# Two sets of transpose DMAs issued from GpSimd's queue, a double block with block sums at the end of branch 2, and a shorter last root

## The chip, the cores and the metric

One core of a Trainium2 chip runs the whole program. The times are device microseconds of that core from one launch. The kernel before has a median of 1646.37 us over three runs (1646.34 to 1649.3). The profile is of one further execution, which took 1648.74 us.

## The reference, cut to what matters

One layer of a hybrid block on x of 256 tokens by 2048 channels, all in float32.

```
h    = rmsnorm(x) ; proj = h @ w_in   -> q, k, v, u, z, xbc, dt, 3 gates (2048 x 13856)
att  = windowed attention(q, k, v)          # 256 x 1024
pool = multi-scale means of u, mixed        # 256 x 1024
y    = Mamba-2 scan(xbc, dt)                # 256 x 2048, four groups of 512 channels
ssm  = per-group rmsnorm(y * silu(z)) * ssm_norm_w
m    = s(g0)*(att @ w_attn_br) + s(g1)*(pool @ w_pool_br) + s(g2)*(ssm @ w_ssm_br)
x    = x + m @ w_out
x    = x + (silu(gu[:, :5632]) * gu[:, 5632:]) @ w_down     # gu = rmsnorm(x) @ w_gate_up
out  = rmsnorm(x) * final_w
```

## The kernel before, in words

Every matrix product is done as three TensorE products of rounded parts (L225 to L227, `three`): a float32 weight is cast to fp32r by ScalarE (`whi`, L142) and what the cast left over is computed by VectorE (`wlo`, L143). A **piece** is such a pair of tiles, 128 by 1024 numbers. It feeds twelve matmuls of 512 columns (two k rows, two token halves, three products). There are five buffers each for `whi` and `wlo`, so ScalarE and VectorE can run at most five pieces ahead of TensorE, and three buffers (`raw`) for the weights as they come from HBM, two pieces each. SP's queue issues the loads of `raw` (L153, L293), in program order, each as soon as a buffer is free.

A block of 512 output columns by all 256 tokens is made in one of two ways. `tokens_block` (L229 on) takes 8 pieces: 96 matmuls. `two_blocks` makes two such blocks at once. Of its eight pairs of k rows, two are done by block sums (Strassen's scheme with seven products: 21 matmuls instead of 24), the other six plainly. The block sums need more of VectorE: sums of weights (`vu`, `sraw`, L304 to L307) and of results (L361 to L364, and the adds after it).

A product's input must have its channels on the partitions, and what VectorE and ScalarE compute has its tokens there. `turn` (L487 to L516) changes that: 16 small DMAs (32 KB each, L497) carry a block into `mid`, two VectorE transposes of 32 by 32 squares follow (`tt`, L502), and then a split in rounded parts. Such a turn is made for the four groups of the state-space output (`y`, into `ssm`), for the four blocks of the merged branches (`m`, into `mp`), for the four residual blocks (`x`, into `x2p`) and for the feed-forward blocks. Before the change the 16 DMAs of `m` stand in GpSimd's queue and all others in SP's, among the weight loads.

The order on each engine comes from a scheduler that takes the program as written. Small jobs (`later`) wait in a list from which `side` takes one after each piece when enough time is held to be spare; `pause(5.0)` or `pause(12.0)` in that list keeps `turn`'s second half away from its first half. Each engine then runs its own instructions strictly in that order, so an instruction that waits holds up all behind it.

The stretch in question: branch 2's gates and products (`two_gates`, `gate`, `branch`), four z blocks (L1016 to L1033: `silu` of z, times `y`, sum of squares, root, scaling at L1027, then `turn`), branch 3's gates (`two_gates(2, 0)`, whose double block begins with a block-sum pair), and `two_branches`, which reads `ssm`. Later come w_out with `residual` (L1056) and the feed-forward part. The last lines (L1143 on) make the final root for each token half and store the output.

Of the kernel before, what the change touches and what calls it, by code (L numbers as in the profile page):

```python
# [10 lines left out]
F32 = mybir.dt.float32  # L11
# [6 lines left out]
D = 2048  # L18
# [53 lines left out]
def hybrid_block(ctx: ExitStack, tc: tile.TileContext, ins, out):  # L72
# [16 lines left out]
    def k4(shape, dt=F32, name="k4"):  # L89
        return work.tile([P, *shape], dt, tag="k4", name=name, bufs=22)  # L90
# [13 lines left out]
    def tr():  # L104
        return ps_tr.tile([P, NB], F32, tag="tr", name="tr")
# [17 lines left out]
    def pause(cost):  # L123
        tasks.append((lambda: None, cost))
# [124 lines left out]
    def plain_loads(w, k0, c0, cols):  # L249
        return lambda i, n: [(lambda r: r[:, :, :], rows(w, k0 + i, n, c0, cols))]  # L250
# [236 lines left out]
    def turn(block, k0, dst, scale=None, queue=sp):  # L487

        mid = k4([4, T, P], F32, "mid")
        dst.waiting.add(k0 // 4)

        def move():
            for i in range(4):
                for j in range(4):
                    queue.dma_start(mid[32 * j:32 * j + 32, i], block[32 * i:32 * i + 32, :, j * P:(j + 1) * P])  # L497

        def parts():
            tt = k4([4, SEQ], F32, "tt")  # L500
            for t in range(T):
                dve.transpose(  # L502
                    tt.rearrange("p k (t i s) -> p t i k s", t=T, i=4)[:, t],
                    mid[:, :, t].rearrange("p i (c k) -> p i k c", k=4),
                )
            if scale is None:
                hi, lo = dst.t[k0 // 4]
                split(tt, hi, lo)
            else:
# [409 lines left out]
    def two_gates(br, j):  # L919

        c0 = C_G + br * D + j * NB
        out = []
        for sums in two_blocks(h, h_forms, w_in, 0, (c0, c0 + NB), KD, False):
            sg = k4([T, NB], F32, "sg")
            for t, (q, more) in enumerate(sums):
                dve.tensor_tensor(more, q, more, ALU.add)
                act.activation(sg[:, t, :], more, AF.Sigmoid, scale=rstd1[:, t:t + 1])
            out.append(sg)
        return out
# [12 lines left out]
    def two_branches(j, sgs):

        for n, sums in enumerate(two_blocks(ssm, s_forms, ins["w_ssm_br"][0], 0, (j * NB, (j + 1) * NB), KD)):
            for t, (q, more) in enumerate(sums):
                dve.tensor_tensor(more, q, more, ALU.add)
                dve.tensor_tensor(more, more, sgs[n][:, t, :], ALU.mult)
                dve.tensor_tensor(m4[j + n][:, t, :], m4[j + n][:, t, :], more, ALU.add)
# [59 lines left out]
    sgs = two_gates(1, 1)  # L1008
    branch(1, 1, po, ins["w_pool_br"][0], sgs[0], [tr(), tr()])
    branch(1, 2, po, ins["w_pool_br"][0], sgs[1], [sm(), sm()])  # L1010
    branch(1, 3, po, ins["w_pool_br"][0], gate(1, 3))


    ssg = tiny([T, GROUPS], "ssg", 1)
    ssm = Parts(KD, "ssm")
    for g in range(GROUPS):  # L1016
        for t, a in enumerate(tokens_block(h, KD, plain_loads(w_in, 0, C_Z + g * NB, NB), NB)):
            sz = k2([NB], F32, "sz")
            act.activation(sz, a, AF.Silu, scale=rstd1[:, t:t + 1])
            dve.tensor_tensor(ys[g][:, t, :], ys[g][:, t, :], sz, ALU.mult)  # L1020
            junk = k2([NB], F32, "junk")
            act.activation(junk, ys[g][:, t, :], AF.Square, accum_out=ssg[:, t, g:g + 1])

        def finish(g=g):
            rstd = rsqrt(ssg[:, :, g], NB, [T], "rsg")
            for t in range(T):
                dve.tensor_scalar(ys[g][:, t, :], ys[g][:, t, :], rstd[:, t:t + 1], None, ALU.mult)  # L1027

        later(finish, 1.5)
        turn(ys[g], 4 * g, ssm, lambda k: norms[:, 0, k:k + 1])  # L1030

        if g == 0:
            s_forms = block_forms(ssm, (0, 1))  # L1033

    sgs = two_gates(2, 0)
    finish_tasks()
# [19 lines left out]
    def residual(j, accs):  # L1056
        for t, a in enumerate(accs):
            dve.tensor_tensor(x2[j][:, t, :], a, x2[j][:, t, :], ALU.add)
            junk = k2([NB], F32, "junk")
            act.activation(junk, x2[j][:, t, :], AF.Square, accum_out=ss2[:, t, j:j + 1])  # L1060
        turn(x2[j], 4 * j, x2p, lambda k: norms[:, 1, k:k + 1])
        if j == 0:
            forms.append(block_forms(x2p, (0, 1)))

# [78 lines left out]
    part = tiny([T], "part", 1)  # L1143
    dve.tensor_reduce(part, ss3, AX.X, ALU.add)
    dve.tensor_scalar(part, part, 1.0 / D, EPS, ALU.mult, ALU.add)
    out_v = out[0].rearrange("(t p) c -> p t c", p=P)
    for t in range(T):
        tok = slice(t * P, (t + 1) * P)
        o = acc()[:, :256]
        for k in range(nk):  # L1150
            hi, lo = wl[k // 4]
            three(o, f.hi(k)[:, tok], f.lo(k)[:, tok], hi[:, k % 4, :], lo[:, k % 4, :], k == 0, k == nk - 1)
        x_ = x2[3][:, t, 256:]
        dve.tensor_tensor(x_, o, x_, ALU.add)
        junk = k2([256], F32, "junk")
        ss = tiny([1], "ss_last")
        dve.scalar_tensor_tensor(junk, x_, 1.0, x_, ALU.mult, ALU.mult, accum_out=ss)
        rstd = rsqrt(ss, D, [1], "rs3", part[:, t:t + 1])
        dve.scalar_tensor_tensor(x_, x_, rstd, fw[7], ALU.mult, ALU.mult)
        sp.dma_start(out_v[:, t, 3 * NB + 256:], x_)  # L1160
        act.mul(x2[3][:, t, :256], x2[3][:, t, :256], rstd)
        act.dma_start(out_v[:, t, 3 * NB:3 * NB + 256], x2[3][:, t, :256])
        for j in range(3):
            if j == 1:
                act.mul(x2[j][:, t, :], x2[j][:, t, :], rstd)
                act.dma_start(out_v[:, t, j * NB:(j + 1) * NB], x2[j][:, t, :])
# [29 lines left out]
```

## Time and profile before

| what | value |
|---|---|
| median of three runs | 1646.37 us |
| the profiled execution | 1648.74 us |
| its span, first to last instruction | 1646.6 us |
| TensorE busy | 1626.4 us, 99% |
| VectorE busy | 1318.8 us, 80% |
| ScalarE busy | 898.2 us, 55% |
| GpSimd busy | 96.8 us, 6% |
| mean granted TensorE clock | 0.998 of 2.4 GHz |

TensorE's matmuls overlap, so its time is better counted in matmuls per stretch than in busy time. The counted stretches are in the rows below. Idle time stands in brackets behind an instruction, with what ended it.

### The profile page before, as it was taken

How to read it: one execution, taken by the hardware profiler on the slowest of the kernel's cores; microseconds unless marked ns; L12 is line 12 of the kernel's file. 1: busy time of each engine (PE TensorE's matmuls, PEld its weight loads, DVE VectorE, ACT ScalarE, POOL GpSimd, SP SyncE). 2: the span in 40 equal slices, each digit the busy share in tenths (PEclk: the TensorE clock that was granted, in tenths of full speed). 3: DMA queues.
4: the chain of work that ended last, by engine and by line, in shares of the span. 5: the costliest groups of instructions: out<-in, count | busy, mean ns of one | idle time of the engine just before them, and what ended most of it. 6: DMA issues, size and time to landing. Idle time of an engine off the chain costs nothing.

```text
span 1646.6 us, 20971 instructions
## 1 busy us (share of the span) xinstructions
PE 1626.4 (99%) x7689; PEld 1349.5 (82%) x7689; DVE 1318.8 (80%) x1738; ACT 898.2 (55%) x1190; POOL 96.8 (6%) x126
## 2 busy tenths in 40 slices
PE   8999999999999999999999999999999999999998
PEld 7888888888888888778888878888888888888887
DVE  5789898964786557688886799988879888888986
ACT  5467678644554457554545565554445555445553
POOL 1000001210220100002230000000000000000000
PEclk9999999999999999999999999999999999999999
DMA  8654566546566556566866666666666666666663
GB/s 250 204 159 146 166 196 205 179 158 200 161 224 212 197 185 212 155 233 203 265 221 191 202 211 226 206 215 215 204 205 193 219 214 217 205 203 199 216 212 103
DMA packets 214088, 328.83 MB, mean 200 GB/s; under 512 B 16253, under 2 KB 86145, under 8 KB 213985
## 3 DMA queue, kind: packets, MB, share of 16 engines
q1 hardware_dynamic: 209056, 317.77, 59.2%
q0 software_dynamic: 4176, 8.86, 1.9%
q8 instruction: 60, 0.98, 0.2%
q10 hardware_dynamic: 752, 0.86, 0.2%
q14 instruction: 44, 0.35, 0.1%
HBM read 313.25 MB, written 2.13 MB: 192 GB/s over the span
## 4 chain that ended last, share of the span: by engine, by line
PE 86%; SPq 4%; DMA 4%; DVE 3%; issue 1%; ACT 1%; DVEq 0%; ACTq 0%
PE acc L225 19%; PE acc L227 19%; PE acc L226 19%; PE acc L383 9%; PE acc L384 4%; SPq L497 4%; PE sm L226 2%; PE tr L227 2%; PE tr L226 2%; PE tr L225 2%; PE sm L225 2%; PE sm L227 2%; DVE wlo L143 1%; DMA raw<-in_w_gate_up_dram 1%; PE sm L868 1%
## 5 line engine op out<-in xcount | busy, mean ns | idle before, releaser
L143 DVE TENSOR_TENSOR wlo<-raw,whi 128x1024 fp32r<-128x1024 f32 (+2 forms) x500 | 600.2, 1215 | 155.8 <-ACT whi L142 154.7
L142 ACT CAST whi<-raw 128x1024 fp32r<-128x1024 f32 (+2 forms) x500 | 509.1, 1035 | 361.9 <-PE acc L227 244.3
L383 PE MATMUL acc<-h,whi 128*128 128x512 f32 x640 | 228.4, 400 | 0.0
L226 PE MATMUL acc<-wlo,x2p_hi 128*128 128x512 f32 x572 | 223.2, 390 | 1.2 <-DVE wlo L143 1.2
L225 PE MATMUL acc<-whi,x2p_hi 128*128 128x512 f32 x572 | 223.3, 390 | 0.0
L227 PE MATMUL acc<-whi,x2p_lo 128*128 128x512 f32 x572 | 223.0, 390 | 0.0
L226 PE MATMUL acc<-wlo,h 128*128 128x512 f32 (+1 forms) x508 | 195.5, 386 | 5.8 <-DVE wlo L143 5.7
L225 PE MATMUL acc<-whi,h 128*128 128x512 f32 (+1 forms) x508 | 196.9, 390 | 2.3 <-ACT whi L142 1.9
L227 PE MATMUL acc<-whi,h 128*128 128x512 f32 (+1 forms) x508 | 194.6, 386 | 0.0
L384 PE MATMUL acc<-h,wlo 128*128 128x256 f32 x640 | 180.3, 282 | 0.0
L142 ACT CAST whi<-sraw 128x1024 fp32r<-128x1024 f32 x84 | 88.1, 1049 | 121.8 <-PE acc L227 96.1
L383 PEld LDWEIGHTS acc<-h,whi 128*128 128x128 f32 x640 | 120.2, 188 | 30.1 <-issue 1.5
L143 DVE TENSOR_TENSOR wlo<-sraw,whi 128x1024 fp32r<-128x1024 f32 x84 | 102.6, 1221 | 45.4 <-ACT whi L142 45.2
L226 PEld LDWEIGHTS acc<-wlo,x2p_hi 128*128 128x128 f32 x572 | 107.4, 188 | 25.0 <-DVE wlo L143 2.3
L227 PEld LDWEIGHTS acc<-whi,x2p_lo 128*128 128x128 f32 x572 | 107.4, 188 | 23.0
L225 PEld LDWEIGHTS acc<-whi,x2p_hi 128*128 128x128 f32 x572 | 107.3, 188 | 23.0
L384 PEld LDWEIGHTS acc<-h,wlo 128*128 128x128 f32 x640 | 120.8, 189 | 1.8 <-issue 1.8
L226 PEld LDWEIGHTS acc<-wlo,h 128*128 128x128 f32 x508 | 95.8, 189 | 26.4 <-DVE wlo L143 7.2
L225 PEld LDWEIGHTS acc<-whi,h 128*128 128x128 f32 x508 | 95.6, 189 | 23.0 <-ACT whi L142 2.1
L227 PEld LDWEIGHTS acc<-whi,h 128*128 128x128 f32 x508 | 95.2, 188 | 19.4
L225 PE MATMUL acc<-whi,f_hi 128*128 128x512 f32 x244 | 95.3, 391 | 0.0
L227 PE MATMUL acc<-whi,f_lo 128*128 128x512 f32 x244 | 95.1, 390 | 0.0
(364 smaller groups left out, 2635.1 us busy)
## 6 DMA issues: line engine op xcount, KB each, us to landing
raw<-in_w_in_dram SPq DMA_DIRECT2D x80, 1024.0 KB, 5.3
raw<-in_w_gate_up_dram SPq DMA_DIRECT2D x132, 512.0 KB, 4.8
raw<-in_w_down_dram SPq DMA_DIRECT2D x62, 512.0 KB, 5.0
sraw<-in_w_gate_up_dram SPq DMA_DIRECT2D x44, 512.0 KB, 4.6
raw<-in_w_in_dram SPq DMA_DIRECT2D x43, 512.0 KB, 4.7
raw<-in_w_ssm_br_dram SPq DMA_DIRECT2D x24, 512.0 KB, 5.6
sraw<-in_w_down_dram SPq DMA_DIRECT2D x20, 512.0 KB, 5.0
raw<-in_w_attn_br_dram SPq DMA_DIRECT2D x8, 1024.0 KB, 5.1
```

What stands on the lines that cost most here:

```text
L142: a = act.copy(hi, src)
L143: b = dve.tensor_tensor(lo, src, hi.bitcast(F32), ALU.subtract)
L225: pe.matmul(o, lhsT=xh, rhs=yh, start=first, stop=False)
L226: pe.matmul(o, lhsT=xh, rhs=yl, start=False, stop=False)
L227: pe.matmul(o, lhsT=xl, rhs=yh, start=False, stop=last)
L383: pe.matmul(accs[c], lhsT=hi[:, j, cols], rhs=a.both(k), start=k == 0, stop=False)
L384: pe.matmul(accs[c][:, :SEQ], lhsT=lo[:, j, cols], rhs=a.hi(k), start=False, stop=k == KD - 1)
L497: queue.dma_start(mid[32 * j:32 * j + 32, i], block[32 * i:32 * i + 32, :, j * P:(j + 1) * P])
L868: pe.matmul(p[:, i * HD:(i + 1) * HD], lhsT=mt[:, i, :], rhs=xdt[:, i, :], start=True, stop=True)
```

## The change

Three edits. The turns of `y` and `x` issue their DMAs from GpSimd's queue, and the pause behind a GpSimd turn is 7.0 instead of 12.0. The last gate block of branch 2 and the first z block, two `tokens_block` products before, become one `two_blocks` product with block sums; the branch product that used that gate follows behind it and accumulates in other banks. For the last root ScalarE takes the sum of squares itself with scale and bias, and one VectorE step of the refinement is folded into a precomputed half.

```diff
@@ turn
         later(move)
-        pause(5.0 if queue is sp else 12.0)
+        pause(5.0 if queue is sp else 7.0)
         later(parts, 3.8)
...
+    def gate_of(sums):
+        sg = k4([T, NB], F32, "sg")
+        for t, (q, more) in enumerate(sums):
+            dve.tensor_tensor(more, q, more, ALU.add)
+            act.activation(sg[:, t, :], more, AF.Sigmoid, scale=rstd1[:, t:t + 1])
+        return sg
...
-    branch(1, 3, po, ins["w_pool_br"][0], gate(1, 3))
...
+    def gated(g, accs, in_place=False):
+        for t, a in enumerate(accs):
+            sz = a if in_place else k2([NB], F32, "sz")
             act.activation(sz, a, AF.Silu, scale=rstd1[:, t:t + 1])
             dve.tensor_tensor(ys[g][:, t, :], ys[g][:, t, :], sz, ALU.mult)
...
-        turn(ys[g], 4 * g, ssm, lambda k: norms[:, 0, k:k + 1])
+        turn(ys[g], 4 * g, ssm, lambda k: norms[:, 0, k:k + 1], pool)
...
+    both = two_blocks(h, h_forms, w_in, 0, (C_G + D + 3 * NB, C_Z), KD, False)
+    sg = gate_of(both[0])
+    for q, more in both[1]:
+        dve.tensor_tensor(more, q, more, ALU.add)
+    gated(0, [more for _, more in both[1]], True)
+    branch(1, 3, po, ins["w_pool_br"][0], sg, [tr(), tr()])
+    for g in range(1, GROUPS):
+        gated(g, tokens_block(h, KD, plain_loads(w_in, 0, C_Z + g * NB, NB), NB))
...
-        turn(x2[j], 4 * j, x2p, lambda k: norms[:, 1, k:k + 1])
+        turn(x2[j], 4 * j, x2p, lambda k: norms[:, 1, k:k + 1], pool)
...
+    halves = tiny([T], "halves", 1)
+    dve.tensor_scalar(halves, part, -0.5, None, ALU.mult)
...
-        rstd = rsqrt(ss, D, [1], "rs3", part[:, t:t + 1])
+        rstd, more = tiny([1], "rs3_r"), part[:, t:t + 1]
+        act.activation(rstd, ss, AF.Sqrt, scale=1.0 / D, bias=more)
+        half, q = tiny([1], "rs3_v"), tiny([1], "rs3_q")
+        dve.tensor_scalar(half, ss, -0.5 / D, halves[:, t:t + 1], ALU.mult, ALU.add)
+        dve.reciprocal(rstd, rstd)
+        dve.scalar_tensor_tensor(q, rstd, half, rstd, ALU.mult, ALU.mult)
+        dve.scalar_tensor_tensor(rstd, q, 1.5, rstd, ALU.add, ALU.mult)
```

SP's queue from the last pool weights of branch 2 to the first weights of branch 3, before. `mid<-y` are the 16 DMAs of a turn, `raw` and `sraw` the weight loads.

```order
L153 DMA raw<-in_w_in_dram 128x4x512 x10
L497 DMA mid<-y 32x2x128 x16
L153 DMA raw<-in_w_in_dram 128x4x512 x5
L497 DMA mid<-y 32x2x128 x16
L153 DMA raw<-in_w_in_dram 128x4x512
L153 DMA raw<-in_w_in_dram 128x2x512 x4
L497 DMA mid<-y 32x2x128 x16
L153 DMA raw<-in_w_in_dram 128x2x512 x2
L293 DMA sraw<-in_w_in_dram 128x2x512 x2
L153 DMA raw<-in_w_in_dram 128x2x512 x5
L497 DMA mid<-y 32x2x128 x16
```

The same stretch after the change.

```order
L153 DMA raw<-in_w_in_dram 128x4x512 x12
L153 DMA raw<-in_w_in_dram 128x2x512 x6
L293 DMA sraw<-in_w_in_dram 128x2x512 x2
L153 DMA raw<-in_w_in_dram 128x2x512 x6
L293 DMA sraw<-in_w_ssm_br_dram 128x2x512 x2
```

No turn stands among the loads any more; in GpSimd's queue the four turns of `y` now stand in one row, ahead of those of `m`, with two sums of branch 2 behind the first.

VectorE's order around the third turn of `y`, before: from the scaling that makes `y` ready (L1027) to the transposes. `wlo<-sraw` and `wlo<-vu` belong to the block-sum pair at the head of branch 3's gates, the `wlo<-raw` behind them is the first plain piece after that pair.

```order
L1027 TENSOR_SCALAR y<-y,rsg_r 128x512 x2
L143 TENSOR_TENSOR wlo<-raw,whi 128x1024
L143 TENSOR_TENSOR wlo<-sraw,whi 128x1024
L307 TENSOR_TENSOR sraw<-sraw 128x512
L143 TENSOR_TENSOR wlo<-vu,whi 128x1024
L143 TENSOR_TENSOR wlo<-sraw,whi 128x1024
L143 TENSOR_TENSOR wlo<-raw,whi 128x1024
L502 STREAM_TRANSPOSE tt<-mid 128x4x4x32 x2
```

The same place after the change.

```order
L1029 TENSOR_SCALAR y<-y,rsg_r 128x512 x2
L143 TENSOR_TENSOR wlo<-raw,whi 128x1024
L143 TENSOR_TENSOR wlo<-sraw,whi 128x1024
L307 TENSOR_TENSOR sraw<-sraw 128x512
L143 TENSOR_TENSOR wlo<-vu,whi 128x1024
L143 TENSOR_TENSOR wlo<-sraw,whi 128x1024
L502 STREAM_TRANSPOSE tt<-mid 128x4x4x32 x2
L143 TENSOR_TENSOR wlo<-raw,whi 128x1024
```

The transposes stand one piece earlier: the first plain piece of the gates is now behind them.

ScalarE's order around the second turn of `y`, before. `ssm_hi` is the split that follows the transposes, `sz` the silu of the third z block (with its table load), `junk` a sum of squares.

```order
L1019 ACT_TABLE_LOAD
L1019 ACTIVATE sz<-acc,rs_r 128x512
L142 CAST whi<-raw 128x1024
L1022 ACTIVATE junk,ssg<-y 128x512
L1019 ACTIVATE sz<-acc,rs_r 128x512
L142 CAST whi<-raw 128x1024
L145 ACTIVATE ssm_hi<-tt,norms 128x256 x4
```

And after the change.

```order
L145 ACTIVATE ssm_hi<-tt,norms 128x256 x4
L1021 ACT_TABLE_LOAD
L1021 ACTIVATE sz<-acc,rs_r 128x512
L142 CAST whi<-raw 128x1024
L1024 ACTIVATE junk,ssg<-y 128x512
L1021 ACTIVATE sz<-acc,rs_r 128x512
L142 CAST whi<-raw 128x1024
```

The split now comes first, so the third z block's silu waits for the second turn.

## Rows read from the trace of the kernel before

**Rows 1.** The page, busy time of each engine.
```profile
PE 1626.4 (99%) x7689; PEld 1349.5 (82%) x7689; DVE 1318.8 (80%) x1738; ACT 898.2 (55%) x1190; POOL 96.8 (6%) x126
```

**Rows 2.** Stretches: us, busy us (x instructions) per engine, clock, DMA share, GB/s.
```profile
core 0: us, PE busy (x) PEld busy (x) DVE busy (x) ACT busy (x) POOL busy (x), PEclk, DMA share, GB/s
660.00:680.00 20.00, 19.41 (x85) 15.58 (x84) 13.54 (x18) 11.65 (x18) 0.00 (x0) 1.00 0.54 174
680.00:700.00 20.00, 18.76 (x82) 15.38 (x83) 13.89 (x20) 11.35 (x13) 0.00 (x0) 1.00 0.44 122
700.00:720.00 20.00, 16.13 (x64) 12.82 (x63) 19.04 (x25) 10.65 (x15) 0.00 (x0) 0.91 0.66 234
720.00:740.00 20.00, 20.00 (x89) 16.44 (x88) 14.76 (x14) 10.93 (x12) 0.00 (x0) 1.00 0.66 224
...
940.00:960.00 20.00, 18.79 (x81) 14.49 (x80) 19.20 (x29) 11.45 (x18) 0.00 (x0) 1.00 0.73 249
...
705.00:710.00 5.00, 3.32 (x10) 2.67 (x11) 5.00 (x7) 2.23 (x3) 0.00 (x0) 0.77 0.52 162
```

**Rows 3.** TensorE's timeline: start, us, instruction, idle time before it and its releaser.
```profile
681.24 0.50 PE L226 MATMUL acc<-wlo,h 128*128 128x512 f32 x1 [1.84 <-DVE wlo L143]
...
706.68 0.50 PE L226 MATMUL acc<-wlo,h 128*128 128x512 f32 x1 [3.87 <-DVE wlo L143]
```

**Rows 4.** SP's queue, third and fourth turn of y.
```profile
659.82 10.77 SPq L497 DMA_DIRECT2D mid<-y  x16
670.68 1.04 SPq L153 DMA_DIRECT2D raw<-in_w_in_dram  x2
...
686.42 11.50 SPq L497 DMA_DIRECT2D mid<-y  x16
```

**Rows 5.** VectorE's timeline around the third and fourth turn.
```profile
658.91 0.88 DVE L1027 TENSOR_SCALAR y<-y,rsg_r 128x512 f32<-128x512 f32 x2
...
672.25 2.06 DVE L502 STREAM_TRANSPOSE tt<-mid 128x512 f32<-128x512 f32 x2 [3.76 <-DMA mid<-y]
...
699.49 1.09 DVE L502 STREAM_TRANSPOSE tt<-mid 128x512 f32<-128x512 f32 x1 [4.88 <-DMA mid<-y]
```

**Rows 6.** Landing of the 16 DMAs of y's fourth turn, from SP.
```profile
DMA to landing us min/median/max: 1.8/1.9/3.6
```

**Rows 7.** GpSimd's timeline, third turn of m.
```profile
847.89 8.51 POOL L497 DMA_DIRECT2D mid<-m  x16 [41.94 <-ACT whi L142]
```

**Rows 8.** Landing of its first five DMAs, then of its last eight.
```profile
DMA to landing us min/median/max: 1.7/1.8/1.8
...
DMA to landing us min/median/max: 4.3/5.6/5.9
```

**Rows 9.** SP's queue beside the same turn.
```profile
852.05 6.09 SPq L153 DMA_DIRECT2D raw<-in_w_out_dram  x6
```

**Rows 10.** VectorE's timeline: a split, six pieces in a row, the wait for m.
```profile
654.90 1.67 DVE L146 SCALAR_TENSOR_TENSOR ssm_lo<-tt,norms,ssm_hi 128x256 fp32r<-128x256 f32 x4
...
765.81 6.90 DVE L143 TENSOR_TENSOR wlo<-raw,whi 128x1024 fp32r<-128x1024 f32 x6
...
861.65 2.06 DVE L502 STREAM_TRANSPOSE tt<-mid 128x512 f32<-128x512 f32 x2 [4.41 <-DMA mid<-m]
```

**Rows 11.** ScalarE's timeline: table load, split behind a turn, a cast.
```profile
645.49 1.28 ACT L1019 ACT_TABLE_LOAD   x1
...
653.30 1.71 ACT L145 ACTIVATE ssm_hi<-tt,norms 128x256 fp32r<-128x256 f32 x4 [2.39 <-DVE tt L502]
...
666.17 1.05 ACT L142 CAST whi<-raw 128x1024 fp32r<-128x1024 f32 x1 [1.67 <-PE acc L227]
```

**Rows 12.** The last root, second token half: VectorE and ScalarE.
```profile
1639.36 0.08 DVE L1157 DVE_READ_ACCUMULATOR junk<-x 128x1 f32 x1
...
1639.73 0.20 ACT L462 ACTIVATE rs_r<-rs_v 128x1 f32<-128x1 f32 x1 [2.18 <-DVE rs_v L461]
...
1640.36 0.16 DVE L465 TENSOR_TENSOR rs_q<-rs_q,rs_v 128x1 f32<-128x1 f32 x1
...
1640.74 0.48 DVE L1159 SCALAR_TENSOR_TENSOR x<-x,rs_r,fw 128x256 f32<-128x256 f32 x1
```

More of the change, by code (lines that the diff above doesn't have):

```diff
@@ L921, in two_gates @@
         c0 = C_G + br * D + j * NB
[L922 to L929, printed above, removed]
+        return [gate_of(sums) for sums in two_blocks(h, h_forms, w_in, 0, (c0, c0 + NB), KD, False)]
+    def gate_of(sums):
[4 more added lines that the diff above has]
+        return sg
     def branch(br, j, a_parts, w, sg, banks=None):
@@ L942, in two_branches @@
     def two_branches(j, sgs):
-        for n, sums in enumerate(two_blocks(ssm, s_forms, ins["w_ssm_br"][0], 0, (j * NB, (j + 1) * NB), KD)):
+        for n, sums in enumerate(two_blocks(ssm, s_forms[0], ins["w_ssm_br"][0], 0, (j * NB, (j + 1) * NB), KD)):
             for t, (q, more) in enumerate(sums):
@@ L1010, in hybrid_block @@
     branch(1, 2, po, ins["w_pool_br"][0], sgs[1], [sm(), sm()])
-    branch(1, 3, po, ins["w_pool_br"][0], gate(1, 3))
     ssg = tiny([T, GROUPS], "ssg", 1)
     ssm = Parts(KD, "ssm")
-    for g in range(GROUPS):
-        for t, a in enumerate(tokens_block(h, KD, plain_loads(w_in, 0, C_Z + g * NB, NB), NB)):
-            sz = k2([NB], F32, "sz")
+    s_forms = []
+    def gated(g, accs, in_place=False):
+        for t, a in enumerate(accs):
+            sz = a if in_place else k2([NB], F32, "sz")
             act.activation(sz, a, AF.Silu, scale=rstd1[:, t:t + 1])
@@ L1022, in hybrid_block, with finish @@
             act.activation(junk, ys[g][:, t, :], AF.Square, accum_out=ssg[:, t, g:g + 1])
-        def finish(g=g):
+        def finish():
             rstd = rsqrt(ssg[:, :, g], NB, [T], "rsg")
@@ L1029, in hybrid_block @@
         later(finish, 1.5)
-        turn(ys[g], 4 * g, ssm, lambda k: norms[:, 0, k:k + 1])
+        turn(ys[g], 4 * g, ssm, lambda k: norms[:, 0, k:k + 1], pool)
         if g == 0:
-            s_forms = block_forms(ssm, (0, 1))
+            s_forms.append(block_forms(ssm, (0, 1)))
+    both = two_blocks(h, h_forms, w_in, 0, (C_G + D + 3 * NB, C_Z), KD, False)
[6 more added lines that the diff above has]
+        gated(g, tokens_block(h, KD, plain_loads(w_in, 0, C_Z + g * NB, NB), NB))
     sgs = two_gates(2, 0)
```

## The prediction

> **What bounds the kernel now.** I read the page first, then stretches of 20 us over the whole span, then TensorE's gaps, and last the queues of SP, VectorE, ScalarE and GpSimd around these gaps. TensorE is busy 99% of the span [rows 1], but matmuls overlap, so I count them: a full stretch holds 89, which is 20 / 89 = 0.225 us each. Only four stretches after the start hold clearly fewer [rows 2]: three from 660 to 720 us with 85 + 82 + 64 = 231, so 60 - 231 x 0.225 = 8.0 us are lost there, and the one from 940 us with 81, so 1.8 us are lost there. Everywhere else TensorE is full; a change can win only by fewer matmuls, by these 9.8 us, or at the two ends.
>
> The gaps end with a `wlo` of VectorE: 1.84 us at 681.24 and 3.87 us at 706.68 [rows 3]. Behind the second the clock falls: from 705 to 710 us it is granted at 0.77 on average, between the two levels of 1.2 and 2.4 GHz [rows 2]. Two things make `wlo` late. SP's queue spends 10.77 and 11.50 us on the 16 DMAs of a turn, and only behind them come the next weight loads [rows 4]. And VectorE waits 3.76 and 4.88 us in front of `tt` for the same DMAs [rows 5]; no piece can be made meanwhile, and ScalarE's split `ssm_hi` waits too [rows 11].
>
> **The change part by part.** *The double block.* Two block-sum pairs take 21 matmuls each instead of 24: 6 x 0.225 = 1.35 us gone. VectorE gets more to do there (sums of weights and results, some 13 us by 1.15 us for 1024 columns [rows 10]) in about 43 us where the gate and z blocks alone used less than half of it; hidden. If the cover were gone, each microsecond would show in full. The block's place also makes the first `y` ready about one branch product earlier.
>
> *The last root.* ScalarE's root waits no longer for the VectorE step behind the accumulator read. In the rows the read starts at 1639.36 and ends at 1639.44, the root starts at 1639.73 and would start at 1639.49: 0.24. One VectorE step of 0.19 goes as well (from 1640.36 to the next): together 0.43 us, on the path that ends the kernel [rows 12]. The step that fills the precomputed half runs beside the root, the other half lies before the last sums.
>
> *The turns.* Eight turns leave SP's queue, so its 10 to 11 us blocks disappear and weights arrive early. What is late next is the turn itself, since VectorE and ScalarE wait in front of the transposes in their fixed order. Let D be the time from a ready block to its last landed DMA. From SP, the third turn of `y` took 672.25 - 659.79 = 12.5 us [rows 5]. From GpSimd I have the third turn of `m`: issue takes 8.51 us [rows 7] (0.53 each), landing 1.8 us at first and 4.3 to 5.9 at the end [rows 8], and VectorE's wait ended 861.65 - 847.89 = 13.8 us after the first issue [rows 10]. The late ones were issued from 852 us on, when six weight loads began [rows 9]. So D lies between 8.51 + 1.8 = 10.3 us (no load in flight) and 13.8 us (loads all the time). I take 11.5, nearer to the free end: while VectorE stands in front of `tt`, it frees no `raw` buffer, so loads stop after the last piece made and the last of the 16 DMAs have the engines nearly alone.
>
> Now the chain, on a clock that is 0 when TensorE ends branch 2 and starts the second z block. One table load is 1.28, a cast 1.05 (about 0.6 for 512 columns, an estimate from it), a split on ScalarE 1.71 [rows 11]; a piece on VectorE 1.15, two transposes 2.06, a split 1.67 [rows 10]; the small steps of a root and the scaling come to 1.6 [rows 5, 12].
> - First `y` ready: the double block ends at -10.8 (four pieces of 2.7 before 0). On ScalarE follow three casts, two table loads, two silus, two squares and a root (8.4), on VectorE 1.6: ready at -0.8.
> - From its landing to the second `y`: transposes, a piece, split, the block sums of `ssm` (4.2), four pieces, a product (14.3), ScalarE's square, silu, cast, square, table and root (4.4), and 1.6: 20.3.
> - From that landing to the third `y`: ScalarE's order has the split ahead of the silu now, so 2.06 + 1.71 and then table, silu, cast, square, silu, cast, square, cast, table, root and 1.6 follow: 13.8.
> - From that landing to the first plain piece of branch 3's gates, which now stands behind the transposes: 2.06 + 1.15 = 3.2.
>
> The piece is there at -0.8 + 20.3 + 13.8 + 3.2 + 3 D = 36.5 + 3 D. TensorE wants it after 24 pieces and a block-sum pair: 64.8 + 21 x 0.225 = 69.5. It waits 3 D - 33: 1.5 us at D = 11.5. The next piece is 5.3 later (a product, the split, `vu`, a product and the piece itself on VectorE) and the one before it lasts 2.7: another 2.6. The fourth turn costs about 0.5. So 4.6 of the 8.0 us stay lost, and 3.4 are won. For the four residual turns the same walk leaves 0.3 of the 1.8 us: their chain has no silu and more plain pieces between; 1.5 won. The turns of `m` have a shorter pause, but their transposes stand at nearly the same pieces and their data has long landed, or is waited for as now; TensorE has no gap there. Cost nothing; if VectorE's lead of five pieces were gone, the 4.41 us wait [rows 10] would show.
>
> Sum: 3.4 + 1.5 + 1.35 + 0.43 = 6.7 us. The profiled execution took 1648.74, 2.4 over the median of 1646.37; taken from the median it gives 1639.7 us.
>
> A rule speaks against such a gain. By the Trainium skill, DMA: Bandwidth & Descriptors, section Issuing engines are not separate DMA queues, issuing from several engines saves only the sequencer's issue time, which is usually small beside the transfer. The trace disagrees on the size: 10.77 us of issue in SP's queue for DMAs that land after 1.9 [rows 4, 6].
>
> **The rivals.** *All gaps closed.* If landing stays near 1.8 us, D is 10.3: 3 D - 33 is negative, the next piece is 0.5 late, and the gain is 7.5 + 1.8 + 1.35 + 0.43 = 11.1: 1635.3 us. For it: the first five DMAs [rows 8]. Against: z blocks load weights steadily. The same page of the Trainium skill (Queues, rings and completion order) says that each DMA engine goes round its queues packet by packet. By that a small DMA would not wait for a whole load, and this rival would hold; landing of 5.6 us beside loads [rows 8] speaks against it.
>
> *Only the sure part.* If VectorE's wait in front of `tt`, not SP's queue, is what starves TensorE, and D comes out near the 12.5 us that it has from SP, the waits of the two stretches stay about as they are, and 1.35 + 0.43 = 1.8 us remain: 1644.6, no change that can be told. This is also what the skill's first rule would give.
>
> *Slower: the third turn becomes the bound.* Three turns stand in one chain in front of one piece, so each microsecond of D costs three there. At D = 13.8, as for `m` [rows 10], the wait is 3 x 13.8 - 33 = 8.4, 6.9 more than in my sum; add about 1 for the lower clock after such a gap (in the stretch from 705 us 10 matmuls were done in 3.32 busy us, where 3.32 / 0.225 is 15: 1.1 us [rows 2]), 1.4 for earlier pieces that come late and the fourth turn, and 0.9 at the residual turns: 6.7 - 10.2 = -3.5, so 1649.9. Each microsecond of D costs about 4.5 in all, so it decides from D = 11.5 + 6.7 / 4.5 = 13.0 on. For it: the one turn measured whole. Against: it ran beside six loads at once.
>
> **How the numbers follow.** What a measurement of this kernel can tell from no change is about 0.2%, 3.3 us: 1643.1 to 1649.7. The forecast (D from 11 to 12.2) has 0.42, all gaps closed 0.20, the sure part (D to 13.8) 0.25, slower by more than that 0.13. So faster 0.62, same 0.25, slower 0.13. The forecast's own range is 1637.5 to 1643; the whole range goes from 1635, where everything is won, to 1648.5, within the third case and part of the fourth.
>
> **What would show it.** In the profile after, SP's queue shows no L497 of `y` or `x`, and GpSimd's 128 more DMAs. The stretches 640 to 720 us hold some 15 matmuls more than now, with a gap of one to three microseconds behind the first block-sum pair of branch 3's gates, ended by a `wlo`, and another a piece later; VectorE's waits in front of `tt` are there still, 2 to 5 us each, now for GpSimd's DMAs. From 940 us on there are 88 or more. The tail from the last matmul is 0.4 us shorter. I am wrong if the first of these gaps is over 5 us (turns of 13 us and more), if it is missing (near 10), or if gaps open in the double block, which I count as covered.

## The result, and the profile after

The changed kernel takes 1656.04 us (median of 4 runs, 1653.84 to 1659.44) against 1646.85 before (a fourth run of it, 1647.33, moved its median from 1646.37): 1.0055, 95% interval 1.0034 to 1.0076. It is slower, where 1639.7 was forecast; the time lies outside the stated range. A second set of runs (E9) gave 1.0044 (1.0032 to 1.0056). The profiled execution has a span of 1655.0 us, 8.4 more than before.

TensorE does the forecast six matmuls less (7683 against 7689) and starts its last one 8.6 us later. The stretches show where, in the columns of [rows 2]; first after, then those of before that [rows 2] does not show.

```profile
620.00:640.00 20.00, 19.73 (x87) 16.05 (x86) 18.61 (x36) 16.20 (x22) 2.78 (x6) 1.00 0.66 215
640.00:660.00 20.00, 19.83 (x87) 16.07 (x87) 10.69 (x14) 10.03 (x17) 5.78 (x11) 1.00 0.58 180
660.00:680.00 20.00, 14.42 (x64) 11.55 (x62) 11.82 (x18) 10.20 (x14) 8.53 (x16) 0.97 0.61 184
680.00:700.00 20.00, 20.00 (x76) 16.17 (x77) 17.41 (x26) 14.18 (x20) 7.17 (x14) 0.85 0.59 184
700.00:720.00 20.00, 18.40 (x81) 14.77 (x81) 15.01 (x19) 8.61 (x13) 1.36 (x3) 1.00 0.58 187
720.00:740.00 20.00, 19.07 (x82) 14.86 (x81) 17.86 (x20) 13.62 (x17) 0.00 (x0) 1.00 0.65 222
...
860.00:880.00 20.00, 19.43 (x85) 15.46 (x84) 12.09 (x12) 7.38 (x8) 12.27 (x23) 1.00 0.77 237
940.00:960.00 20.00, 20.00 (x90) 16.45 (x89) 13.27 (x20) 9.85 (x14) 8.53 (x16) 1.00 0.71 231
960.00:980.00 20.00, 18.03 (x78) 14.16 (x77) 17.01 (x22) 11.46 (x15) 0.00 (x0) 1.00 0.47 157
1000.00:1020.00 20.00, 19.61 (x87) 15.85 (x86) 17.89 (x25) 10.69 (x12) 0.00 (x0) 1.00 0.88 307
1020.00:1040.00 20.00, 19.63 (x86) 15.55 (x85) 18.74 (x26) 10.81 (x12) 0.00 (x0) 1.00 0.34 107
1040.00:1060.00 20.00, 18.36 (x79) 14.30 (x78) 15.58 (x17) 9.84 (x12) 0.00 (x0) 1.00 0.81 278
675.00:680.00 5.00, 0.10 (x1) 0.10 (x1) 3.30 (x4) 1.22 (x4) 0.00 (x0) 0.90 0.00 1
680.00:685.00 5.00, 5.00 (x12) 3.74 (x13) 5.00 (x9) 4.86 (x10) 0.00 (x0) 0.50 0.00 0
```

```profile
620.00:640.00 20.00, 20.00 (x90) 16.57 (x89) 17.57 (x35) 16.01 (x23) 0.00 (x0) 1.00 0.68 227
640.00:660.00 20.00, 20.00 (x90) 16.57 (x89) 15.16 (x24) 13.94 (x21) 0.00 (x0) 1.00 0.68 227
...
860.00:880.00 20.00, 20.00 (x90) 16.57 (x89) 15.65 (x14) 9.52 (x10) 6.65 (x13) 1.00 0.72 222
960.00:980.00 20.00, 20.00 (x89) 16.36 (x88) 19.88 (x24) 13.41 (x16) 0.00 (x0) 1.00 0.82 279
1000.00:1020.00 20.00, 20.00 (x89) 16.44 (x88) 19.38 (x29) 11.26 (x14) 0.00 (x0) 1.00 0.72 248
1020.00:1040.00 20.00, 20.00 (x89) 16.40 (x89) 18.31 (x21) 10.56 (x12) 0.00 (x0) 1.00 0.50 143
1040.00:1060.00 20.00, 20.00 (x89) 16.45 (x88) 17.59 (x19) 10.98 (x12) 0.00 (x0) 1.00 0.85 305
```

Counted against the same stretches of before, at 0.225 us a matmul: 620 to 740 us (called the stretch of `y` below) holds 477 instead of 500 (5.2 us lost), 860 to 880 holds 85 instead of 90 (1.1), 940 to 980 holds 168 instead of 170 (0.4), 1000 to 1060 holds 252 instead of 267 (3.4). Less 1.35 for the six matmuls and 0.28 for the tail that is 8.5 us, the 8.4 of the spans.

The first big gap is where the prediction put it, one matmul behind the first block-sum pair of branch 3's gates, but longer than [rows 3]:

```profile
679.90 0.80 PE L226 MATMUL acc<-wlo,h 128*128 128x512 f32 x1 [5.58 <-DVE wlo L143]
```

Until 685.6 us the clock is then at its lower level (0.50 from 680 to 685 in the windows), and 13 matmuls take 0.427 us each instead of 0.227: 2.6 us more. VectorE had stood 7.40 us in front of the third turn's transposes (3.76 in [rows 5]), and GpSimd's 16 DMAs of this turn show why. First VectorE, from the ready `y` on, then GpSimd, then the weight loads in SP's queue, then the landing of these 16 DMAs and of all 64 of `y` (to be set against [rows 7, 8]):

```profile
663.00 0.89 DVE L1029 TENSOR_SCALAR y<-y,rsg_r 128x512 f32<-128x512 f32 x2
...
676.70 2.04 DVE L502 STREAM_TRANSPOSE tt<-mid 128x512 f32<-128x512 f32 x2 [7.40 <-DMA mid<-y]
```

```profile
664.46 5.87 POOL L497 DMA_DIRECT2D mid<-y  x11 [17.09 <-ACT whi L142]
671.29 2.67 POOL L497 DMA_DIRECT2D mid<-y  x5 [0.97 <-DMA mid<-y]
```

```profile
660.39 5.84 SPq L153 DMA_DIRECT2D raw<-in_w_in_dram  x4
669.33 0.89 SPq L293 DMA_DIRECT2D sraw<-in_w_in_dram  x2
684.94 3.82 SPq L153 DMA_DIRECT2D raw<-in_w_in_dram  x4
```

```profile
DMA to landing us min/median/max: 2.6/3.9/5.6
...
DMA to landing us min/median/max: 1.7/4.3/6.8
```

Issue takes 8.5 us and one wait of 1 us for an earlier DMA of the same turn, and landing 4 us, not 1.9. From ready `y` to transposes the four turns take 14.3, 13.6, 12.8 and 14.6 us; from SP they took 11.9, 11.7, 12.5 and 13.1.

The tail is shorter, from the accumulator read to the last scaling of the second token half 1.10 us instead of 1.38 [rows 12]:

```profile
1647.99 0.08 DVE L1170 DVE_READ_ACCUMULATOR junk<-x 128x1 f32 x1
...
1648.44 0.16 DVE L1176 RECIPROCAL rs_r<-rs_r 128x1 f32<-128x1 f32 x1
...
1649.09 0.48 DVE L1179 SCALAR_TENSOR_TENSOR x<-x,rs_r,fw 128x256 f32<-128x256 f32 x1
```

### The profile page after: what moved, and what is told of

The parts are those of the page before. It is cut to its first block, busy times and chain, and to the rows that moved or that the text cites. A ratio compares the mean times of both kernels' runs of the same rounds, so it can differ in the third digit from the quotient of the medians.

```text
span 1655.0 us, 21013 instructions
## 1 busy us (share of the span) xinstructions
PE 1629.1 (98%) x7683; PEld 1348.9 (82%) x7683; DVE 1329.8 (80%) x1755; ACT 899.7 (54%) x1195; POOL 164.3 (10%) x254
## 4 chain that ended last, share of the span: by engine, by line
PE 49%; DVE 3%; DMA 2%; SPq 1%; issue 1%; POOL 1%; ACT 0%; DVEq 0%; ACTq 0%; POOLq 0%
PE acc L226 14%; PE acc L227 14%; PE acc L225 14%; PE tr L227 1%; PE tr L226 1%; PE tr L225 1%; PE sm L226 1%; PE sm L227 1%; PE sm L225 1%; SPq L497 1%; DVE wlo L143 1%; POOL mid L497 1%; DMA mid<-x 1%; DMA mid<-m 0%; DVE tt L502 0%
## 5 line engine op out<-in xcount | busy, mean ns | idle before, releaser
L143 DVE TENSOR_TENSOR wlo<-raw,whi 128x1024 fp32r<-128x1024 f32 (+2 forms) x496 | 592.7, 1211 | 122.6 <-ACT whi L142 120.9
L142 ACT CAST whi<-raw 128x1024 fp32r<-128x1024 f32 (+2 forms) x496 | 502.8, 1034 | 317.8 <-PE acc L227 215.6
L226 PE MATMUL acc<-wlo,h 128*128 128x512 f32 (+1 forms) x496 | 191.9, 388 | 7.7 <-DVE wlo L143 7.6
L225 PE MATMUL acc<-whi,h 128*128 128x512 f32 (+1 forms) x496 | 192.2, 390 | 1.6 <-ACT h L145 0.7
L227 PE MATMUL acc<-whi,h 128*128 128x512 f32 (+1 forms) x496 | 190.3, 387 | 0.0
L142 ACT CAST whi<-sraw 128x1024 fp32r<-128x1024 f32 x88 | 92.5, 1051 | 124.8 <-PE acc L227 94.5
L143 DVE TENSOR_TENSOR wlo<-sraw,whi 128x1024 fp32r<-128x1024 f32 x88 | 107.7, 1223 | 47.2 <-ACT whi L142 47.1
L225 PEld LDWEIGHTS acc<-whi,h 128*128 128x128 f32 x496 | 93.6, 189 | 22.0 <-ACT h L145 2.0
L227 PEld LDWEIGHTS acc<-whi,h 128*128 128x128 f32 x496 | 93.3, 189 | 18.8 <-DVE h L146 0.2
L502 DVE STREAM_TRANSPOSE tt<-mid 128x512 f32<-128x512 f32 x46 | 47.7, 1069 | 61.8 <-DMA mid<-y 24.2
L226 PE MATMUL acc<-wlo,f_hi 128*128 128x512 f32 x244 | 95.1, 390 | 0.0
```

The lines of the kernel that those rows point to most:

```text
L142: a = act.copy(hi, src)
L143: b = dve.tensor_tensor(lo, src, hi.bitcast(F32), ALU.subtract)
L225: pe.matmul(o, lhsT=xh, rhs=yh, start=first, stop=False)
L226: pe.matmul(o, lhsT=xh, rhs=yl, start=False, stop=False)
L227: pe.matmul(o, lhsT=xl, rhs=yh, start=False, stop=last)
L502: dve.transpose(tt.rearrange("p k (t i s) -> p t i k s", t=T, i=4)[:, t], mid[:, :, t].rearrange("p i (c k) -> p i k c", k=4),)
```

## The experiments

My theory after the result: a turn issued from GpSimd is too long beside weight loads, and the waits on it stand in one chain (theory A in the expectations). Its rivals: the place of the transposes in VectorE's order (B), and a loss that only comes later, at `m` and `x` (C). All kernels are the changed one with the edit shown, but for E7. Ratios are to the kernel before, run on the same chip, with 95% intervals.

**E1 to E3, which queue.** `pool` is taken away from the turns named; the pause of `m` is 12.0.

```diff
-        turn(ys[g], 4 * g, ssm, lambda k: norms[:, 0, k:k + 1], pool)      # E1, E3
+        turn(ys[g], 4 * g, ssm, lambda k: norms[:, 0, k:k + 1])
-        turn(x2[j], 4 * j, x2p, lambda k: norms[:, 1, k:k + 1], pool)      # E1, E2
+        turn(x2[j], 4 * j, x2p, lambda k: norms[:, 1, k:k + 1])
-        pause(5.0 if queue is sp else 7.0)                                 # E1, E2, E3
+        pause(5.0 if queue is sp else 12.0 if scale is None else 7.0)
```

> The changed kernel with the turns of y and x back in SP's queue, pauses as before; the double block and the shorter last root stay. Theory A (the turn issued from GpSimd is too long: 12.8 to 14.6 us from a ready y to its transposes, against 12.5 from SP): the gaps are those of the kernel before (8.0 us from 660 to 720, 1.8 from 940) and only six matmuls (1.35 us) and 0.28 us of the tail are gone: 1645.2 us, about 0.999. Theory B (what counts is where the transposes stand in VectorE's order; all four of y stand here at the same pieces as in the changed kernel): TensorE loses about 14 us there as in the changed kernel, 1651 us, about 1.0025.

Measured 1648.47 us, 1.0004 (0.9995 to 1.0013). VectorE's order up to the third turn's transposes is that of the changed kernel, but its turns take 12.4, 11.8, 12.9 and 12.5 us. The third turn is no shorter than in the changed kernel (12.9 against 12.8), and VectorE waits as long in front of it (7.50 against 7.40); but the first two are 3.8 us shorter together, so the third begins earlier against TensorE, and TensorE's gap is 2.98 us instead of 5.58:

```profile
671.71 2.04 DVE L502 STREAM_TRANSPOSE tt<-mid 128x512 f32<-128x512 f32 x2 [7.50 <-DMA mid<-y]
```

```profile
674.91 0.50 PE L226 MATMUL acc<-wlo,h 128*128 128x512 f32 x1 [2.98 <-DVE wlo L143]
```

So the queue makes the difference, by way of the chain, and theory B as the main cause is out. The 1.6 us of the sure part do not show: 620 to 740 us holds 497 matmuls, 3 fewer than before, 940 to 960 holds 77 instead of 81. What the new order may cost by itself is of that size.

> The changed kernel with the turns of x alone back in SP's queue; y stays on GpSimd's, the pause of m is 12.0 as before. Theory A: y's stretch loses about 14 us as in the changed kernel, 6 more than before, the stretch behind the residual 1.8 as before: 1651.3 us, about 1.0027. Theory C (the loss comes from later, GpSimd's queue being late for m or x because y's turns stand in it): y's stretch loses no more than 8, 1645 us.

Measured 1652.09 us, 1.0026 (1.0017 to 1.0035), 3.6 us more than E1: theory A's time. The profile alone would not show it. The stretch of `y` holds 487 here, 13 fewer than before, where theory A expected some 27 fewer, and E3, with `y` on SP, holds 488. One execution differs from the next: with the changed order and `y` on GpSimd six profiles hold 464 to 487 (478 on average: E2, E4, E9, E10, E14 and the changed kernel), with `y` on SP four hold 487 to 497 (492: E1, E3, E11, E15). The averages are 3.3 us apart, as the times are.

> The changed kernel with the turns of y alone back in SP's queue; x stays on GpSimd's, the pause of m is 12.0 as before. Theory A: y's stretch loses 8.0 us as before, the stretch from 940 us about 5 instead of 1.8: 1645.2 + 3.2 = 1648.4 us, about 1.001. Theory C: the residual's stretch loses no more than before, 1645 us.

Measured 1645.67 us, 0.9985 (0.9976 to 0.9994): neither. Moving x alone wins 0.19% against E1, and 940 to 980 us holds 178 matmuls, which is full. So the loss behind `x` in the changed kernel is not from the queue of x by itself.

**E4, the pause of m.** Only the pause line is that of E1; `y` and `x` stay on GpSimd's queue.

> The changed kernel with the pause behind m's turns at 12.0 as before; the turns of y and x stay on GpSimd's queue with 7.0. The changed kernel is 1.0055 of before, while y alone on GpSimd's queue cost 1.0026 and x alone gave 0.9985. Theory P (the missing 3 to 5 us come from the shorter pause of m, which changes the order behind it: in the changed kernel alone SP's second turn of the feed-forward blocks stands between the two halves of a block-sum load, and 1040 to 1060 us hold 79 matmuls; with 12.0 it stands behind both): 1646.9 + 6.5 = 1653.5 or less, 1.004 or lower, with 89 matmuls from about 1040 to 1060. Theory Q (the two moves together do it, because y's late stretch leaves TensorE without its lead for x): 1656, 1.0055 as now.

Measured 1648.16 us, 1.0007 (0.9997 to 1.0017), from 860 to 1060 us no matmul is missing. That is the sum of E2 and E3, each taken from E1. The shorter pause of `m`, which I had priced at nothing, is the largest part of the loss: 0.37 to 0.48% (1.0044 and 1.0055 against 1.0007).

**E5 to E8 and E13, the length of a turn.** In E5 GpSimd and SP take turns in issuing; the pause of `m` is 12.0.

```diff
-                    queue.dma_start(mid[32 * j:32 * j + 32, i], block[32 * i:32 * i + 32, :, j * P:(j + 1) * P])
+                    q = queue[j % 2] if isinstance(queue, tuple) else queue
+                    q.dma_start(mid[32 * j:32 * j + 32, i], block[32 * i:32 * i + 32, :, j * P:(j + 1) * P])
...
-        turn(ys[g], 4 * g, ssm, lambda k: norms[:, 0, k:k + 1], pool)
+        turn(ys[g], 4 * g, ssm, lambda k: norms[:, 0, k:k + 1], (pool, sp))
-        turn(x2[j], 4 * j, x2p, lambda k: norms[:, 1, k:k + 1], pool)
+        turn(x2[j], 4 * j, x2p, lambda k: norms[:, 1, k:k + 1], (pool, sp))
```

> The changed kernel with the 16 DMAs of each turn of y and x issued half by GpSimd and half by SP; the pause of m is 12.0 as before. Issue takes 8 x 0.54 to 0.60 = 4.3 to 4.8 us on each queue instead of 8.5 to 10.5. Theory A: with landing of 2 to 5 us a turn takes 8 to 10 us from the ready y, so that VectorE's waits in front of the transposes shrink and the gaps of both stretches come to less than 3 us together: about 1646.9 - 9.8 + 2 - 1.6 = 1637.5 us, 0.994. Theory B (the transposes stand three pieces behind their y here instead of four to five, which is 8 us of TensorE's work, so VectorE waits for them as long as now): 1650 us or more.

Measured 1634.98 us (1634.95 to 1635.77), 0.9922 (0.9909 to 0.9936), the best of all kernels here. Turns of `y` take 8.6 at most, 7.6, 6.8 and 6.7 us, and TensorE has no gap, though the transposes stand even nearer to their `y` in VectorE's order. Two stretches of its windows, the third turn's wait, SP's queue at that turn, and the landing from GpSimd and from SP:

```profile
660.00:680.00 20.00, 20.00 (x90) 16.44 (x89) 16.21 (x22) 14.92 (x23) 0.00 (x0) 1.00 0.60 187
680.00:700.00 20.00, 20.00 (x90) 16.45 (x88) 17.44 (x25) 11.93 (x16) 4.26 (x8) 1.00 0.68 213
```

```profile
661.75 2.06 DVE L503 STREAM_TRANSPOSE tt<-mid 128x512 f32<-128x512 f32 x2 [2.46 <-DMA mid<-y]
```

```profile
654.99 5.09 SPq L498 DMA_DIRECT2D mid<-y  x8
660.18 1.05 SPq L153 DMA_DIRECT2D raw<-in_w_in_dram  x2
```

```profile
DMA to landing us min/median/max: 1.8/2.2/3.7
...
DMA to landing us min/median/max: 1.8/2.3/3.9
```

The same queue of GpSimd lands its DMAs of `y` after 2.2 us here and after 4.3 us in the changed kernel: while SP issues its half, no weight load starts. For `x` this does not hold: its DMAs in E5 land after a median of 4.6 us from GpSimd and 4.8 from SP.

> As the kernel with both sets of turns half on each queue, but the turns of x are back in SP's queue alone. If the loss in y's stretch and the one behind the residual are separate: no gap from 600 to 740 us, 81 or fewer matmuls in the 20 us around 940, so 1635.0 + 1.8 to 3 = 1637 to 1638 us, 0.9935. If a y stretch without loss also gives the residual its lead back, 1635 us as with both.

Measured 1637.47 us, 0.9943 (0.9930 to 0.9956): the two stretches are separate; y's half turns are worth most, x's some 2.5 us more (by the medians; the intervals of E5 and E6 overlap a little).

E7 is the kernel before with E5's edit; a pause of 5.0 behind the half turns.

> The kernel before, without the double block and the shorter root, with the turns of y and x issued half by GpSimd and half by SP. If the length of the turns is all: no gaps in either stretch, and the time is that of the changed kernel with half turns plus six matmuls (1.35 us) and the tail (0.28 us): 1636.6 us, 0.993. If the double block is needed because its earlier first y gives the chain its start: gaps of 2 us or more stay in y's stretch and the time is 1639 us or more.

Measured 1638.42 us, 0.9944 (0.9931 to 0.9958). Against E5 that is 3.4 us (1.6 expected, which the intervals allow): without gaps the double block is worth its matmuls. y's stretch holds 529, where E5 has 539, so its earlier start may help a little; the other pause (5.0, not 7.0) was not separated from it.

> The changed kernel with the turns of y issued from ScalarE's queue, to measure how long a 32 KB DMA takes to land beside weight loads when it comes from neither SP nor GpSimd. Theory L (landing is long because weight loads are in flight at the same time): median 3.5 us or more, as from GpSimd (4.3). Theory G (GpSimd's own way of issuing makes it long): 1.9 us as from SP. ScalarE cannot cast while it issues (16 x about 0.6 = 9.6 us per turn), so the time is worse than the changed kernel's in either case, 1660 us or more; only the landing counts here.

One run, with `act` for `pool` at `y`: 1661.88 us; landing 2.7 us (1.9 to 5.9), between the two theories; ScalarE's late casts may also have held back loads. Sorted by the loads beside each DMA, the trace does lean to L: the 29 of the 64 DMAs beside which loads moved less than 20 GB/s (packets of 2 KB and more in SP's queue) landed after a median of 1.9 us, the 26 beside which they moved over 120 GB/s after 4.0.

E13 has `(pool, pool, pool, sp)` for `y`.

> The kernel with half turns, but of y's 16 DMAs GpSimd issues 12 and SP 4; x stays half and half. A turn of y should take 12 x 0.54 = 6.5 us of issue and 3 to 4 of landing, about 10.5 us from the ready y, between the 7 with halves and the 12.8 to 14.6 with all 16. The chain of the prediction (TensorE waits 3 D - 33 us, so nothing below D = 11): at most 1 us lost in y's stretch, 1635 to 1637 us, 0.993. If the loss grew evenly with D instead (12 to 14 us at 13.7, none at 7): 6 to 7 us lost, 1641 us, 0.9965.

Measured 1646.42 us, 0.9992 (0.9983 to 1.0001): neither, and worse than both. The turns took 12.5, 12.7, 10.8 and 11.4 us, not 10.5, and y's stretch holds 500, as before. From 860 to 900 us, in front of the splits of `m`, 169 matmuls stand instead of 180, 2.5 us, which was not followed up. SP's four DMAs, with loads right behind them in the same queue, landed like this, where all 16 from SP had 1.9 us [rows 6]:

```profile
DMA to landing us min/median/max: 1.9/3.4/4.9
```

That goes with E8: it isn't GpSimd's way of issuing alone; DMAs from SP land late too, as soon as loads are let in beside them. E13 is no clean test of the chain's length, though: the transposes of its third turn stand a piece earlier than in the changed kernel, and TensorE's gap stands in front of another matmul, the last piece of the block-sum pair:

```profile
674.22 0.50 PE L226 MATMUL sm<-wlo,forms 128*128 128x512 f32 x1 [4.66 <-DVE wlo L143]
```

**E9 to E12 and E14 to E16, why the pause costs.** E9 is the changed kernel again. E10 and E12 change one number of it; E11, E14 and E15 keep its pause of 7.0 and take `pool` from both, from `x` and from `y`; E16 is E5 with 7.0 for `m`.

```diff
-        pause(5.0 if queue is sp else 7.0)
+        pause(4.5 if queue is sp else 7.0)      # E10
+        pause(5.0)                              # E12
```

> The changed kernel once more, on the same chip as the next three. 1.0055 of before, about 1655 us; its losses in matmuls lie at 620 to 740, 860 to 880, 960 to 980 and 1000 to 1060 us.

Measured 1653.91 us, 1.0044 (1.0032 to 1.0056).

> The changed kernel with the pause of SP's turns (here the feed-forward turns alone) at 4.5 instead of 5.0. Nothing differs before the first feed-forward turns; in SP's queue the second of them stands behind the pair of block-sum loads again, not between its halves. Theory W (that place is a large part of what the shorter pause of m costs): the 17 matmuls that are missing from 1000 to 1060 us are back, 3.8 us: 0.0023 below the changed kernel of this call, about 1.003. Theory O (the loss comes from m's and x's transposes waiting earlier, and the place in SP's queue only shows it): about 1.0055 still.

Measured 1653.81 us, 1.0042 (1.0029 to 1.0055). The matmuls from 1000 to 1060 us are back (267), but the time is that of E9. Theory W, that this place is a large part, has no support in the times; a part of 2 us is within the intervals, and the table below shows one in the profiles.

> The changed kernel with the turns of y and x back in SP's queue and the pause of m at 7.0 as changed (the run with y and x on SP and 12.0 gave 1.0004). SP's queue has the second feed-forward turn behind the pair of loads here. Theory W: 1.0004 to 1.001, the pause does nothing by itself. Theory O: 1.004 to 1.005, 7 us lost from 860 to 1060 us.

Measured 1648.79 us, 1.0011 (1.0003 to 1.0020): W's side, with turns of y and x on SP the pause costs next to nothing.

> The changed kernel with the pause of all turns from GpSimd at 5.0 instead of 7.0, y's transposes at the same pieces; SP's queue has the second feed-forward turn behind the pair of loads. Theory W: as with 12.0 or with the mended place, 1.001 to 1.003. Theory O (a shorter pause makes transposes wait longer): as bad as the changed kernel or worse, 1.0055 or more.

Measured 1653.89 us, 1.0040 (1.0028 to 1.0052): between the two. The place is mended here too (89 and 90 matmuls from 1020 to 1060 us), but another gap, of 1.81 us, opened at 1008 us, where 20 us hold 79; so this says little on W.

> The changed kernel with x's turns alone back in SP's queue, m's pause 7.0 as changed (with 12.0 this gave 1.0026). Theory R (the shorter pause costs only where x's turns come from GpSimd): 1.0026 to 1.0035. Theory Y (it costs where TensorE comes out of y's stretch without its lead): 1.0055 to 1.0065.

Measured 1656.14 us, 1.0046 (1.0033 to 1.0059): between R and Y.

> The changed kernel with y's turns alone back in SP's queue, m's pause 7.0 as changed (with 12.0 this gave 0.9985). Theory R: the shorter pause costs 4 to 6 us here, 1.001 to 1.002, with matmuls missing from 940 to 1060 us. Theory Y: 0.9985 to 0.9995.

Measured 1652.71 us, 1.0029 (1.0018 to 1.0040): R, and more than it said. VectorE in E3 and then in E15 (same stretch, the pause the only difference), and TensorE in E15:

```profile
933.47 2.08 DVE L502 STREAM_TRANSPOSE tt<-mid 128x512 f32<-128x512 f32 x2 [0.54 <-DMA mid<-x]
936.58 1.28 DVE L1069 TENSOR_TENSOR x<-acc,x 128x512 f32<-128x512 f32 x2
```

```profile
934.04 2.07 DVE L502 STREAM_TRANSPOSE tt<-mid 128x512 f32<-128x512 f32 x2 [3.97 <-DMA mid<-x]
...
939.97 1.28 DVE L1069 TENSOR_TENSOR x<-acc,x 128x512 f32<-128x512 f32 x2
```

```profile
940.71 0.50 PE L225 MATMUL acc<-shi,forms 128*128 128x512 f32 x1 [1.33 <-DVE x L1069]
```

With 7.0 the transposes of x's third turn stand one piece earlier in VectorE's order, and the sum of the last residual block one piece later. VectorE waits 3.97 us in front of the transposes instead of 0.54, and that sum is 3.4 us later: TensorE waits for its banks, and the last turn starts late.

> Both sets of turns half on each queue, m's pause 7.0 instead of 12.0. SP's second feed-forward turn stands between the halves of a block-sum load here, as in the changed kernel. Theory R': with turns of 7 us VectorE keeps its lead and neither the pause nor that place costs anything: 1635 us, 0.9925. If the pause costs by itself: 1639 to 1641 us.

Measured 1637.48 us, 0.9937 (0.9924 to 0.9951): between the two, 2.5 us more than E5, in the profile all of it in one stretch (1020 to 1040 us), which holds 78 matmuls. SP's queue there, and VectorE behind it:

```profile
1011.00 0.37 SPq L293 DMA_DIRECT2D sraw<-in_w_gate_up_dram  x1
1011.71 11.59 SPq L498 DMA_DIRECT2D mid<-ff  x16
1023.34 0.59 SPq L293 DMA_DIRECT2D sraw<-in_w_gate_up_dram  x1
```

```profile
1024.69 2.06 DVE L503 STREAM_TRANSPOSE tt<-mid 128x512 f32<-128x512 f32 x2 [3.46 <-DMA mid<-ff]
1027.37 1.23 DVE L304 TENSOR_TENSOR vu<-sraw 128x1024 f32<-128x1024 f32 x1 [0.63 <-DMA sraw<-in_w_gate_up_dram]
```

A feed-forward turn stands between the two halves of a load. VectorE first waits 3.46 us in front of that turn's transposes, and then the block sums of the weights wait 0.63 us more for the second half. The same place, in the changed kernel, in E9 and in E15, has 79, 79 and 81 matmuls in 20 us; where it is mended (E10) 89.

| y, x from | m's pause 12.0 | m's pause 7.0 | 7.0 against 12.0, behind the 3800th matmul |
|---|---|---|---|
| SP, SP | 1.0004 (E1) | 1.0011 (E11) | 0.6 us |
| GpSimd, SP | 1.0026 (E2) | 1.0046 (E14) | 1.0 us |
| SP, GpSimd | 0.9985 (E3) | 1.0029 (E15) | 5.6 us |
| GpSimd, GpSimd | 1.0007 (E4) | 1.0055, 1.0044 (changed, E9) | 7.3 us, 4.6 us; E10 2.7 us |
| half, half | 0.9922 (E5) | 0.9937 (E16) | 2.7 us |

The two columns of ratios come from different chips, each against the kernel before on its own chip. The last column is from the profiles, one execution each: the time from the start of the 3800th matmul to that of the last, less the same time with 12.0. The two kernels of a row have the same order on every engine up to 806 us at least, where the transposes of the first turn of `m` stand, and the 3800th matmul starts at 755 to 773 us; so the pause cannot have caused what differs before it. In E14 that is most: 5.0 of the 6.0 us between its profile and E2's lie before it. Behind it the pause costs where the turns of `x` come from GpSimd or where the feed-forward turn stands between two halves of a load, as theory R and W together have it: E10's 2.7 us (`x` alone) and E16's 2.7 (that place alone) make about E15's 5.6.

## Why the prediction was wrong

The sum forecast 6.7 us won, and the profile has 8.4 lost. Of these 15.1 us, 8.6 lie in the stretch of `y` (3.4 to be won, 5.2 lost), 6.4 behind it (1.5 to be won, 4.9 lost) and 0.15 at the last root.

- **What bounds the kernel** was read rightly: TensorE is full but for the waits of the two stretches, and with these gone (E5) the kernel is 12.9 us faster than before.
- **The double block and the root.** Six matmuls went. The root gave 0.28 us, not 0.43: it starts 0.25 us earlier but takes 0.29 instead of 0.20, and the steps behind it wait for it.
- **The turns of y: the step that failed first is the choice of D.** I took 11.5 us, "nearer to the free end", because loads should stop while VectorE stands before the transposes. They did stop, but too late: the four turns took 13.8 us on average, the upper bound, at a median landing of 4.3 us, and even the third, in front of which VectorE stood longest, took 12.8. The chain itself held, nearly to the tenth. On its clock the first `y` was ready at -0.6 instead of -0.8; the way from a landing to the next `y` or to the piece took 20.15, 13.65 and 3.15 us instead of 20.3, 13.8 and 3.2; with the measured 40.7 us for three turns the piece was there at 77.1, where 36.5 + 40.7 makes 77.2. TensorE wanted it at 71.6, not 69.5, as its matmuls took 0.227 us and two small gaps came before; so it waited 5.58 us and not 7.7, and lost 2.6 more at the lower clock. In E1, E3, E2 and E4 the same sum gives 4.1, 4.2, 5.8 and 6.8 us, and the gaps are 2.98, 3.07, 4.67 and 4.95; with 23.0 (E5) it has no wait, and there is none. The rival of the slower side worked its price out from just this D: 13.9 us lost, 5.9 more than before; measured 5.2 more (5.0 on average of the six profiles). A first gap over 5 us with turns of 13 us and more was also named beforehand as the sign of being wrong.
- **The rule of the Trainium skill** in DMA: Bandwidth & Descriptors, Queues, rings and completion order, by which each DMA engine goes round its queues packet by packet, stood behind the rival that all gaps close. The runs say nothing against that rule, only against what was drawn from it, that a small DMA then lands after about 1.8 us: it took 4.3 us beside loads and 2.2 with few of them (E5).
- **The turns of x** gave what was forecast or more, with the old pause of `m`: 1.5 us forecast, about 3 measured (E3 against E1).
- **The pause of m: the step that failed most behind y's stretch.** I wrote "Cost nothing", since the transposes of `m` stand at nearly the same pieces and TensorE had no gap there. Only the turns of `m` were looked at. The pause moves all that stands behind it in VectorE's and SP's orders: transposes of x a piece earlier (E15), a feed-forward turn into the middle of a load (E16). Against 12.0 it costs 0.07% with y and x on SP (within the noise), 0.20% with y and 0.44% with x on GpSimd. With both there it turned 1.0007 into 1.0044 to 1.0055, 6 to 8 us; in the profiles 4.6 to 7.3 us of that lie behind the first instruction that the pause moves.
- **Left open** is how this divides between the two places. The profiles give the feed-forward one 2 to 2.7 us (78 to 81 matmuls instead of 89 to 90), and with it mended (E10) the part behind the 3800th matmul is 1.9 us shorter than in E9; the medians of E9 and E10 do not differ. Why E14 was late before anything in its order differs is open too: it is one execution, on another chip than E2.

## What to carry to other kernels

A transfer in front of a wait in an in-order engine is priced by its whole length beside the traffic that will really run then, not by the landing of its first DMAs; here 16 small DMAs of `y` cost 13.8 us from one queue beside loads and 7.4 from two queues. By the Trainium skill, DMA: Bandwidth & Descriptors, Issuing engines are not separate DMA queues, a second engine saves only issue time. The trace agrees for about 4.4 of these 6.4 us (9.5 us of issue with its pause, against 5.1); the other 2.1 are landing, 4.3 against 2.2 us, because SP's half kept the loads out of the way. All of it was worth 13 us of the kernel (E5 against E4) because a chain of waits hung on it. And a changed delay in a planner's list is an edit to everything behind it: read the new order as far as the next stage, above all where turns stand next to loads that belong together.

## What was not expected of the hardware

- A 32 KB DMA of a turn lands after about 2 us when hardly any weight load runs beside it and after 3.4 us (SP, E13), 4.0 us (ScalarE, E8) or 4.3 us (GpSimd, the changed kernel) when loads do.
- GpSimd issued 16 such DMAs in 8.5 us but stopped for about 1 us or more within nearly every turn (0.97 us behind the eleventh above). This is the program's doing and not the engine's: in the trace its DMAs use eight semaphores in turn, each DMA first waits for the semaphore that it will raise itself, and every such stop ends with the landing of the DMA eight places before. At 0.54 us of issue, eight places are 4.3 us, so a stop comes as soon as landing takes longer than that.
- Behind gaps of 5.58, 4.66 (E13) and 2.98 us (E1) TensorE's clock stood at its lower level for 3 to 6 us. Behind one of 2.25 us (E1) and one of 2.75 us (E11) the windows show it at 1.00; in E11 a second gap, of 2.30 us, followed 3 us of matmuls later, and from 682 to 684 us the clock was granted at 0.50.
